# Mean squares and norm of a gate moved ahead of the first step of queries and keys, its norm weights into the second and third step

## The chip, the core and the metric

The kernel runs on one core of a Trainium2 chip. The metric is the device time of one execution in microseconds (us). The engines of a core work side by side, each through its own queue in order, and wait for one another by semaphores: PE (TensorE, matmuls), ACT (ScalarE), DVE (VectorE), POOL (GpSimd) and SP (which here only issues DMAs).

## What is computed

One decoder block on 1024 tokens of width 1024 in float32: eight heads of attention with a forget gate beside eight groups of a chunked spatial gate, then a gated MLP with a short convolution. The part that matters here, cut from the reference:

```
xn = rmsnorm(h, norm_mix_g)
proj = xn @ w_in                      # q, k, v (512 each), u, vg (512 each), 8 forget columns
log_f = log_sigmoid(proj[..., G_END:] + b_forget)
att = forgetting_attention(q, k, v, log_f)
uv = gelu(proj[..., V_END:G_END])     # u and vg
# chunked_spatial_gating, 8 groups of 64 columns:
vg = rmsnorm(vg, v_gain)              # mean square over the 64 columns of a group
mixed = einsum('gij,bnjgd->bnigd', tril(w_s), chunks_of_128(vg)) + b_s
sg = u * mixed
h = h + concat([att, sg]) @ w_out
```

The change touches the `rmsnorm` of `vg`: squares, their sums by group, the root, its reciprocal, the product with it (the norm) and the product with `v_gain` (the norm weights).

## The kernel before

The big products are done by Strassen-Winograd: matrices are cut into 2 x 2 blocks and seven block products take the place of eight (A11, A12, A22, S1 to S4 against B11, B21, T4, T1, T2, T3, B22). Each float32 operand is split into a high part and a low part (fp32r), and a product of two of them is three matmuls. A split is a cast on ACT and a subtraction on DVE (`split_w`, `tsplit`).

The order of the work around the change is this. First come the products for u, vg and the values (lines around 256), with a gelu on ACT at their end; `vgt[1]` and `vgt[0]` hold the two halves of vg (tokens 512 to 1023 and 0 to 511), each 128 partitions x 4 tiles x 512 columns, in G tiles. Then `forget` multiplies out the eight forget columns (L483), and `forget_sums` turns them into the running sums of log_f: L494 brings them into place, DVE and ACT alternate through the log-sigmoid (Exp, Ln), L507 and L508 multiply by a triangle and by ones, and a run of small adds on DVE follows.

Then come the four steps of queries and keys, `qk_step(i)` for i = 0 to 3, one for each 128 columns of weights. A step is seven products of 12 matmuls each (all on L400): qb (S2), qc (S3), qa (A12, for i > 0; its first product, A11, was made in the step before), qd (S1), qc again (A22, added onto the first), qa of the next step (A11), qd again (S4). Between them DVE combines the results out of PSUM. A product that adds onto qc or qd has to wait until DVE has read the bank. `emit` scales a result, splits it and stores it in `qd` or `kd` for the attention; its stores go out on SP. `nxt_of(i)` loads the next step's weights and makes their sums on POOL.

The gate's norm hangs in these steps. `gate_part(i)` of step i takes a quarter of vg: ACT squares 128 x 1024 elements into a pt tile, DVE sums them by groups of 64 into `gms`; in every second step ACT and DVE make root and reciprocal of 32 means, and one DVE instruction of 128 x 2048 elements norms the whole half. So half 1 is normed in step 1 and half 0 in step 3. `gate_gain(hf)` multiplies a half by the norm weights, 128 x 2048 in one instruction: half 1 in step 3, half 0 after the loop. The weights come by a DMA into a gg tile, issued at the first call.

After the loop, `vgs` splits the normed gate (eight casts into H tiles on ACT, eight subtractions on DVE), the second half of the values is multiplied out (`tmul` and `tprod`, L256, 96 matmuls), and `spatial` does the chunked gate (L661 to L663).

Who goes first is not simply the order of the code. A planner goes through the instructions in that order as their priority, simulates the engines with durations of its own, and on each engine takes the foremost instruction whose inputs and buffers are there; so an instruction can be put ahead of others that stand before it in the code if its engine would be idle. The result is a fixed queue for each engine. Tiles of one tag share a few buffers in turn: pt has three (used by `xu`, one for each step, by the squares and by a row of `scale_row`), gg two (`forget` uses both until `forget_sums` is done; one is used for the sums of each step's weights), H four, G four. All DVE and ACT instructions of this stretch are recorded under L43, a wrapper that also keeps them behind the end of the values' first part. So rows are told apart by their tiles: `gms<-pt` is the sum of squares, `gms<-gms` the root or reciprocal, `G<-G,gms` the norm, `G<-G,gg` the norm weights, `pt<-G` (ACT) the squares, `H<-G,H` the low part of the normed gate.

Of the kernel before, what the change touches and what calls it, by code (L numbers as in the profile page):

```python
# [11 lines left out]
AF = mybir.ActivationFunctionType  # L12
ALU = mybir.AluOpType
AX = mybir.AxisListType
P = 128
# [49 lines left out]
def block_kernel(ctx: ExitStack, tc: tile.TileContext, xT, xtok, wuv, wv, wqk, wf, cpk, bfv,  # L65
                 ggain, g2r, gfr, wsp, woa, wos, wup, wdn, out):
    nc = tc.nc
    act, dve, pool, pe, sp = Line(nc.scalar, tc), Line(nc.vector, tc), Line(nc.gpsimd, tc), nc.tensor, nc.sync
# [13 lines left out]
    def nm(s):  # L82
        uid[0] += 1
        return f"{s}_{uid[0]}"
# [6 lines left out]
    def sb(tag, shape, dt=F32):  # L91
        return (raws if tag == "raw" else late if tag in LATE else early).tile(shape, dt, tag=tag, bufs=BUFS[tag], name=nm(tag))
# [7 lines left out]
    def sbank():  # L100
        return psa.tile([P, 512], F32, tag="s", name=nm("ps"))

    def f32(ap):
        return ap.bitcast(F32)
# [6 lines left out]
    eps = cst.tile([P, 1], F32, name="eps")  # L111
# [85 lines left out]
    def ring(dt=F32R):  # L197
        rn[0] += 1
        return sb(RTAG[(rn[0] - 1) % 6], [P, 2, 512], dt)

    def psq(tag):
        return psa.tile([P, 512], F32, tag="b" if tag in "ab" else "s", bufs=4, name=nm("q" + tag))
# [29 lines left out]
    for p_ in range(2):  # L232
        t = sb("G", [P, 2, 2, 512])
# [3 lines left out]
    vgt = [sb("G", [P, 4, 512]) for _ in range(2)]  # L237
# [91 lines left out]
    for j in range(2):  # L329
        g = gb[2 * j:2 * j + 2]  # L330
# [64 lines left out]
    def product(ps, w, n, first):  # L395
        c = 0
        for k in range(4):
            ks = slice(k * P, (k + 1) * P)
            for wi, xi in ((0, 0), (0, 1), (1, 0)):
                pe.matmul(ps, w[:, wi, ks], xs(n, xi, k), start=(first and c == 0), stop=(c == 11),  # L400
                          skip_group_check=True)
                c += 1
# [85 lines left out]
    def forget_sums(c, r, zr):  # L488
        sel, bfb, z, e, rows = c[0:64, 128:136], c[:, 136:144], c[:, 144:208], c[:, 208:272], c[0:64, 272:400]
        tri, ones, lh, ll = r[:, 0:P], r[:, P:2 * P], r[:, 256:320], r[:, 320:384]  # L490
        v3 = lambda t: t.rearrange("p (h t) -> p h t", h=8)
        ps = sbank()
        for tt in range(8):
            pe.matmul(ps[:, tt * 8:(tt + 1) * 8], zr[:, tt * P:(tt + 1) * P], sel, start=True, stop=True)  # L494
        dve.tensor_tensor(out=v3(z), in0=ps[:, 0:64].rearrange("p (t h) -> p h t", h=8),
                          in1=rstd1.unsqueeze(1).to_broadcast((P, 8, 8)), op=ALU.mult)
        dve.tensor_tensor(out=v3(z), in0=v3(z), in1=bfb.unsqueeze(2).to_broadcast((P, 8, 8)), op=ALU.add)
        dve.scalar_tensor_tensor(out=e, in0=z, scalar=-1.0, in1=z, op0=ALU.mult, op1=ALU.max)
        act.activation(e, e, AF.Exp, scale=-1.0)
        act.activation(e, e, AF.Ln, bias=one[:, 0:1])  # L500
        dve.tensor_scalar(out=z, in0=z, scalar1=-1.0, scalar2=0.0, op0=ALU.mult, op1=ALU.max)
        dve.tensor_tensor(out=z, in0=z, in1=e, op=ALU.add)
        dve.tensor_copy(lh, z)
        dve.tensor_tensor(out=ll, in0=z, in1=f32(lh), op=ALU.subtract)

        for o, m in ((64, tri), (128, ones)):
            pe.matmul(ps[:, o:o + 64], m, lh, start=True, stop=False)  # L507
            pe.matmul(ps[:, o:o + 64], m, ll, start=False, stop=True)  # L508
        whole, run = v3(ps[:, 128:192]), v3(e)
        dve.memset(run[:, :, 0:1], 0.0)  # L510
        for tt in range(1, 8):
            dve.tensor_tensor(out=run[:, :, tt:tt + 1], in0=run[:, :, tt - 1:tt], in1=whole[:, :, tt - 1:tt], op=ALU.add)
        dve.tensor_tensor(out=v3(z), in0=v3(ps[:, 64:128]), in1=run, op=ALU.add)
        pe.transpose(ps[0:64, 192:320], z, ident)
        act.activation(rows, ps[0:64, 192:320], AF.Copy, scale=-1.0)
        sp.dma_start(out=ncd.rearrange("h (t p) -> (h t) p", p=P), in_=rows)
# [4 lines left out]
    def emit(t, dst, i, scale, parts):  # L521
        for o in parts:
            dve.scalar_tensor_tensor(out=t[:, 1, o], in0=t[:, 1, o], scalar=scale, in1=rb[:, o],
                                     op0=ALU.mult, op1=ALU.mult)
            act.copy(t[:, 0, o].bitcast(F32R), t[:, 1, o])
            dve.tensor_tensor(out=t[:, 1, o], in0=t[:, 1, o], in1=t[:, 0, o], op=ALU.subtract)
            for j in range(2):
                sp.dma_start(out=dst[2 * i + j].rearrange("s d t -> d s t")[:, :, o], in_=t[j * 64:(j + 1) * 64, :, o])

    gms = cst.tile([P, 64], F32, name="gms")  # L530

    def gate_part(i):

        hf, t = 1 - i // 2, 2 * (i % 2)
        sq = sb("pt", [P, 2, 512])
        act.activation(sq, vgt[hf][:, t:t + 2, :], AF.Square)
        r = gms[:, hf * 32 + t * 8:hf * 32 + t * 8 + 16]
        dve.tensor_reduce(out=r, in_=sq.rearrange("p t (g d) -> p (t g) d", d=64), axis=AX.X, op=ALU.add)
        if t:
            r = gms[:, hf * 32:hf * 32 + 32]  # L540
            act.activation(r, r, AF.Sqrt, bias=eps[:, 0:1], scale=1.0 / 64)
            dve.reciprocal(r, r)
            v3 = vgt[hf].rearrange("p t (g d) -> p (t g) d", d=64)
            dve.tensor_tensor(out=v3, in0=v3, in1=r.unsqueeze(2).to_broadcast((P, 32, 64)), op=ALU.mult)

    def nxt_of(i):
        if i == 3:
            while True:
                yield None
        w = Weights(i + 1)  # L550
        W.append(w)
        yield None
        w.split("A11")
        yield q1(i + 1, "a")
        w.sums()
        w.split("S2", "S3", "A12")
        w.last_sum()
        yield None
        yield None

    def qk_step(i, qa, nxt):
        w, t = W[i], xu[i]
        x1, u2 = t[:, 0, :], t[:, 1, :]
        qb = psq("b")
        product(qb, w.w["S2"], "T2", True)
        next(nxt)
        dve.tensor_tensor(out=u2, in0=qb, in1=x1, op=ALU.subtract)
        qc = psq("c")
        product(qc, w.w["S3"], "T3", True)
        dve.tensor_tensor(out=tk[:, 1, hi], in0=u2, in1=qc, op=ALU.subtract)  # L570
        w.split("S1")
        if i > 0:
            product(qa, w.w["A12"], "B21", False)
            act.copy(tq[:, 1, lo], qa)
        else:
            dve.tensor_tensor(out=tq[:, 1, lo], in0=q2, in1=x1, op=ALU.add)
        emit(tq, qd, i, -0.125, (lo,))
        w.split("A22")
        if i == 3:
            gate_gain(1)  # L580
        qd_ = psq("d")
        product(qd_, w.w["S1"], "T1", True)
        dve.tensor_tensor(out=tk[:, 1, hi], in0=tk[:, 1, hi], in1=qd_, op=ALU.subtract)
        gate_part(i)
        product(qc, w.w["A22"], "T4", False)
        dve.tensor_tensor(out=tk[:, 1, lo], in0=u2, in1=qc, op=ALU.subtract)
        emit(tk, kd, i, 1.0, (lo, hi))
        qa = next(nxt)
        w.split("S4")
        next(nxt)  # L590
        product(qd_, w.w["S4"], "B22", False)
        dve.tensor_tensor(out=tq[:, 1, hi], in0=qd_, in1=u2, op=ALU.subtract)
        emit(tq, qd, i, -0.125, (hi,))
        return qa

    gg = []

    def gate_gain(hf):
        if not gg:
            gg.append(sb("gg", [P, 512]))  # L600
            sp.dma_start(out=gg[0], in_=ggain.to_broadcast((P, 512)))
        dve.tensor_tensor(out=vgt[hf], in0=vgt[hf], in1=gg[0].unsqueeze(1).to_broadcast((P, 4, 512)), op=ALU.mult)

    W[0].split("S2", "S3")
    forget_sums(*fg)
    for i in range(4):
        qa = qk_step(i, qa, nxt_of(i))

# [2 lines left out]
    for k in range(4):  # L611
        t = sb("raw", [P, 2, 512])
# [4 lines left out]
    w0 = [tsplit(wvr[k][:, 0, :], True) for k in range(4)]  # L617


    gate_gain(0)  # L620
    vgs = [sb("H", [P, 2, 2, 8, 64], F32R) for _ in range(4)]
    for hf in (1, 0):
        for c in range(4):
# [18 lines left out]
    for p_ in range(2):  # L642
        t = ring(F32)
# [207 lines left out]
    def ut_(pool_, tag, shape, dt, bufs):  # L851
        return pool_.tile(shape, dt, tag=tag, bufs=bufs, name=nm(tag))
# [309 lines left out]
    for p_, n in ((upl, "B11"), (upl, "T2"), (upl, "B21"), (upl, "T3"), (upr, "T1"), (upr, "T4"), (upr, "B22")):  # L1162
        t = ut_(p_, "x" + n, [P, 2, 4, 512], F32, 1)
# [168 lines left out]
```

## Time and profile before

| | |
|---|---|
| median of 3 runs | 1097.8 us (1097.66 to 1100.26) |
| the profiled execution | 1102.1 us, span 1100.4 us |
| mean granted TensorE clock | 0.992 |
| busy | PE 97%, DVE 82%, ACT 52%, POOL 23% of the span |
| the four steps of queries and keys | about 118 to 198 us |

A row of a timeline gives start, duration, engine, line, operation, output <- inputs, shapes and count; a bracket at its end is the time that the engine sat idle before it, and who ended the wait. A row of a group has the count behind x, then busy time and mean ns of one, then idle time before. A row of a table of windows has start:end and length, then for PE, PEld, DVE, ACT and POOL the busy time (and instructions), then the granted TensorE clock (1.00 is full), the DMA engines' busy share and GB/s. In the page's line of shares of the chain, "issue" is time in which the engine waited for nothing that is recorded.

### The profile page before, as it was taken

Reading aid. Unit: us, or ns where it says so; the run is one execution under the profiler, and the core shown is the slowest. Engines: PE = TensorE matmul, PEld = TensorE weight load, DVE = VectorE, ACT = ScalarE, POOL = GpSimd, SP = SyncE. Lnnn points to the kernel's source line nnn. Section 1 sums busy time; section 2 is a strip of 40 time slices with the busy share of each in tenths; the row PEclk is TensorE's granted clock in tenths of the full one; section 3 lists DMA queues with packets and bytes.
Section 4 is the critical chain, followed back from the end, with each engine's and each line's share of the span. In section 5 each row is a group of like instructions: output and inputs, shape, how many; then the busy total and the mean of one; then the engine's idle time right before and its main releaser. Section 6 shows DMA issues by size and latency. Waiting matters only on the chain.

```text
span 1100.4 us, 14437 instructions
## 1 busy us (share of the span) xinstructions
PE 1070.2 (97%) x5013; PEld 880.7 (80%) x5013; DVE 897.8 (82%) x1355; ACT 572.2 (52%) x991; POOL 248.6 (23%) x205
## 2 busy tenths in 40 slices
PE   9999999999998999998999999999999999999997
PEld 6888787777877888776888888888888888888886
DVE  5985799775678859999898989999998875898774
ACT  5666544454467856653444444444444454454653
POOL 0002243133144341334232423333232000000000
PEclk9999999999998999999999999999999999999999
DMA  9242366836576345223133232313321898433342
GB/s 329 96 137 94 97 171 181 254 121 215 189 221 171 97 133 185 86 67 134 68 105 134 85 107 96 126 67 125 115 96 46 268 336 301 140 96 103 125 135 97
DMA packets 64713, 158.18 MB, mean 144 GB/s; under 512 B 7672, under 2 KB 7936, under 8 KB 64640
## 3 DMA queue, kind: packets, MB, share of 16 engines
q1 hardware_dynamic: 64352, 156.70, 43.7%
q8 instruction: 39, 0.64, 0.2%
q10 hardware_dynamic: 288, 0.56, 0.1%
q14 instruction: 34, 0.28, 0.1%
HBM read 114.95 MB, written 42.27 MB: 143 GB/s over the span
## 4 chain that ended last, share of the span: by engine, by line
PE 69%; DVE 7%; ACT 3%; issue 2%; DMA 2%; POOL 1%; SPq 0%; ACTq 0%; POOLq 0%; DVEq 0%
PE k L1189 18%; PE qa L999 10%; PE qd L999 10%; PE qc L999 10%; PE qb L999 5%; PE pb L759 3%; PE ps L256 2%; PE pb L749 2%; PE pf L803 1%; PE pf L804 1%; PE pf L802 1%; DMA x<-ncd 1%; PE ps L730 1%; PE ps L729 1%; DVE whb L159 1%
## 5 line engine op out<-in xcount | busy, mean ns | idle before, releaser
L1189 PE MATMUL k<-whb,wha 128*128 128x512 f32 x924 | 209.7, 389 | 0.0
L1189 PEld LDWEIGHTS k<-whb,wha 128*128 128x128 f32 x924 | 173.5, 188 | 36.1
L999 PE MATMUL qa<-xB,wha 128*128 128x512 f32 x528 | 128.9, 393 | 5.8 <-DVE wha L159 5.8
L999 PE MATMUL qc<-xT,whb 128*128 128x512 f32 x540 | 130.2, 390 | 1.4 <-DVE xT L930 1.4
L999 PEld LDWEIGHTS qa<-xB,wha 128*128 128x128 f32 x528 | 100.0, 190 | 27.4 <-DVE wha L159 6.6
L999 PEld LDWEIGHTS qc<-xT,whb 128*128 128x128 f32 x540 | 101.2, 188 | 23.2 <-DVE xT L930 1.8
L153 ACT CAST wha<-sg 128x512 fp32r<-128x512 f32 x77 | 47.9, 622 | 97.8 <-PE k L1189 87.0
L153 ACT CAST whb<-sg 128x512 fp32r<-128x512 f32 x85 | 51.9, 615 | 69.9 <-PE qc L999 67.7
L159 DVE TENSOR_TENSOR wha<-sg,wha 128x512 fp32r<-128x512 f32 x77 | 53.0, 690 | 40.8 <-ACT wha L153 40.6
L159 DVE TENSOR_TENSOR whb<-sg,whb 128x512 fp32r<-128x512 f32 x85 | 63.0, 743 | 9.1 <-ACT whb L153 8.9
L759 PE MATMUL pb<-pt,V 128*128 128x256 f32 (+1 forms) x320 | 59.4, 303 | 7.0 <-ACT pt L750 4.8
L999 PE MATMUL qd<-xB,whb 128*128 128x512 f32 x264 | 63.8, 389 | 0.1
L999 PE MATMUL qd<-xT,whb 128*128 128x512 f32 x264 | 63.4, 389 | 0.0
L759 PEld LDWEIGHTS pb<-pt,V 128*128 128x128 f32 x320 | 48.3, 194 | 18.6 <-ACT pt L750 11.5
L999 PE MATMUL qb<-xT,whb 128*128 128x512 f32 x252 | 61.0, 389 | 1.0 <-DVE whb L159 1.0
L750 ACT CAST pt<-pb 128x512 fp32r<-128x512 f32 (+1 forms) x80 | 40.8, 545 | 33.4 <-PE pb L749 32.7
L999 PEld LDWEIGHTS qd<-xB,whb 128*128 128x128 f32 x264 | 49.5, 188 | 10.7 <-issue 0.5
L999 PEld LDWEIGHTS qd<-xT,whb 128*128 128x128 f32 x264 | 49.6, 188 | 10.3
L751 DVE TENSOR_TENSOR pt<-pb,pt 128x512 fp32r<-128x512 f32 (+1 forms) x80 | 48.2, 632 | 10.9 <-ACT pt L750 10.2
L887 POOL TENSOR_TENSOR sg<-sg,raw 128x512 f32<-128x512 f32 x21 | 42.5, 2022 | 64.1 <-issue 61.6
L999 PEld LDWEIGHTS qb<-xT,whb 128*128 128x128 f32 x252 | 47.2, 188 | 11.1 <-DVE whb L159 1.4
L886 POOL TENSOR_TENSOR sg<-raw 128x512 f32<-128x512 f32 x21 | 30.6, 1458 | 110.0 <-DVE whb L159 85.6
(378 smaller groups left out, 2308.2 us busy)
## 6 DMA issues: line engine op xcount, KB each, us to landing
raw<-wup SPq DMA_DIRECT2D x44, 512.0 KB, 3.6
sg<-hx SPq DMA_DIRECT2D x77, 256.0 KB, 3.0
hx<-hs SPq DMA_DIRECT2D x44, 256.0 KB, 2.0
hx<-ca SPq DMA_DIRECT2D x33, 256.0 KB, 2.0
xT<-wdn SPq DMA_DIRECT2D x28, 256.0 KB, 4.8
raw<-wqk SPq DMA_DIRECT2D x8, 512.0 KB, 3.6
qd<-G SPq DMA_DIRECT2D x16, 256.0 KB, 4.7
kd<-G SPq DMA_DIRECT2D x16, 256.0 KB, 3.2
```

The source lines that it names most:

```text
L153: act.copy(h, src)
L159: return eng.tensor_tensor(out=l, in0=src, in1=f32(h), op=ALU.subtract)
L256: pe.matmul(banks[m], xs(n, xi, k)[:, ms], w[:, wi, :], start=(first and k == 0 and c == 0), stop=(k == 3 and c == 2), skip_group_check=True)
L729: pe.matmul(ps[:, 0:e - c], A[:, qs], B[:, c:e], start=True, stop=False)
L749: pe.transpose(ptr[:, c:c + P], tj[jj][:, k * P:(k + 1) * P], ident)
L750: act.copy(pt[:, 0, 0:w], ptr[:, 0:w])
L751: dve.tensor_tensor(out=pt[:, 1, 0:w], in0=ptr[:, 0:w], in1=f32(pt[:, 0, 0:w]), op=ALU.subtract)
L759: pe.matmul(po[:, oo:oo + n], lhs, pt[:, s, o:o + n], start=(k == 0 and s == 0), stop=(s == 1 and half))
L886: pool.tensor_tensor(out=s[0], in0=a21, in1=a22, op=ALU.add)
L887: pool.tensor_tensor(out=s[1], in0=s[0], in1=a11, op=ALU.add)
L999: pe.matmul(ps, w[:, wi, ks], xb[:, xi, k, :], start=(first and n == 0), stop=(n == 11), skip_group_check=True)
L1189: pe.matmul(banks[bk + m], xh[:, xi, ms], wh[:, wi, :], start=(first and p_ == 0 and n == 0), stop=(p_ == NP - 1 and n == 2), skip_group_c ...
```

## The change

`gate_part` becomes `gate_norm(hf)`, which does all of a half at once: two squares and two sums, root and reciprocal of the 32 means, and the norm as two instructions of 128 x 1024. It is called for half 1 ahead of `forget_sums` and for half 0 behind it, both ahead of the first step. `gate_gain` becomes two instructions of 128 x 1024 for each half; half 1 gets it in step 1 and half 0 in step 2, behind the subtraction of qd. The arithmetic is the same.

```diff
-    def gate_part(i):
-        hf, t = 1 - i // 2, 2 * (i % 2)
-        sq = sb("pt", [P, 2, 512])
-        act.activation(sq, vgt[hf][:, t:t + 2, :], AF.Square)
-        r = gms[:, hf * 32 + t * 8:hf * 32 + t * 8 + 16]
-        dve.tensor_reduce(out=r, in_=sq.rearrange("p t (g d) -> p (t g) d", d=64), axis=AX.X, op=ALU.add)
-        if t:
-            r = gms[:, hf * 32:hf * 32 + 32]
-            act.activation(r, r, AF.Sqrt, bias=eps[:, 0:1], scale=1.0 / 64)
-            dve.reciprocal(r, r)
-            v3 = vgt[hf].rearrange("p t (g d) -> p (t g) d", d=64)
-            dve.tensor_tensor(out=v3, in0=v3, in1=r.unsqueeze(2).to_broadcast((P, 32, 64)), op=ALU.mult)
+    def gate_norm(hf):
+        for t in (0, 2):
+            sq = sb("pt", [P, 2, 512])
+            act.activation(sq, vgt[hf][:, t:t + 2, :], AF.Square)
+            dve.tensor_reduce(out=gms[:, hf * 32 + t * 8:hf * 32 + t * 8 + 16],
+                              in_=sq.rearrange("p t (g d) -> p (t g) d", d=64), axis=AX.X, op=ALU.add)
+        r = gms[:, hf * 32:hf * 32 + 32]
+        act.activation(r, r, AF.Sqrt, bias=eps[:, 0:1], scale=1.0 / 64)
+        dve.reciprocal(r, r)
+        for t in (0, 2):
+            v3 = vgt[hf][:, t:t + 2, :].rearrange("p t (g d) -> p (t g) d", d=64)
+            dve.tensor_tensor(out=v3, in0=v3, in1=r[:, t * 8:t * 8 + 16].unsqueeze(2).to_broadcast((P, 16, 64)), op=ALU.mult)
...
     def qk_step(i, qa, nxt):
...
         w.split("A22")
-        if i == 3:
-            gate_gain(1)
         qd_ = psq("d")
         product(qd_, w.w["S1"], "T1", True)
         dve.tensor_tensor(out=tk[:, 1, hi], in0=tk[:, 1, hi], in1=qd_, op=ALU.subtract)
-        gate_part(i)
+        if i in (1, 2):
+            gate_gain(2 - i)
         product(qc, w.w["A22"], "T4", False)
...
     def gate_gain(hf):
...
-        dve.tensor_tensor(out=vgt[hf], in0=vgt[hf], in1=gg[0].unsqueeze(1).to_broadcast((P, 4, 512)), op=ALU.mult)
+        for t in (0, 2):
+            v = vgt[hf][:, t:t + 2, :]
+            dve.tensor_tensor(out=v, in0=v, in1=gg[0].unsqueeze(1).to_broadcast((P, 2, 512)), op=ALU.mult)
 
     W[0].split("S2", "S3")
+    gate_norm(1)
     forget_sums(*fg)
+    gate_norm(0)
     for i in range(4):
         qa = qk_step(i, qa, nxt_of(i))
...
-    gate_gain(0)
     vgs = [sb("H", [P, 2, 2, 8, 64], F32R) for _ in range(4)]
```

## The prediction

> **What bounds the kernel now.** I read the page first, then TensorE's own order of work around the change, then VectorE's for the same stretch.
>
> ```profile
> span 1100.4 us, 14437 instructions
> PE 1070.2 (97%) x5013; PEld 880.7 (80%) x5013; DVE 897.8 (82%) x1355; ACT 572.2 (52%) x991; POOL 248.6 (23%) x205
> PE 69%; DVE 7%; ACT 3%; issue 2%; DMA 2%; POOL 1%; SPq 0%; ACTq 0%; POOLq 0%; DVEq 0%
> ```
>
> TensorE is busy for 97% of the span and carries 69% of the chain that ended last. Work of other engines is worth only what it makes TensorE wait. So I looked for TensorE's waits in the four steps of queries and keys (118 to 198 us), and found them in the last of them, step 3:
>
> ```profile
> 181.39 2.88 PE L400 MATMUL qa<-x,whl 128*128 128x512 f32 x12
> 184.11 2.88 PE L400 MATMUL qd<-H,whl 128*128 128x512 f32 x12
> 187.69 3.01 PE L400 MATMUL qc<-V,whl 128*128 128x512 f32 x12 [0.70 <-DVE G L43]
> 193.67 4.23 PE L400 MATMUL qd<-t,whl 128*128 128x512 f32 x12 [2.98 <-DVE G L43]
> 219.89 0.39 PE L661 MATMUL pb<-H,wy 128*128 128x512 f32 x1
> ```
>
> One product of 12 matmuls takes 184.11 - 181.39 = 2.72 us start to start. From 184.11 to the first spatial matmul there are three products and the second values product of 96 matmuls, 11 times 12: 29.92 us at that rate. They took 35.78. The loss is 5.86 us, of which 0.70 + 2.98 = 3.68 are waits for VectorE. Most of the other 2.18 is clock:
>
> ```profile
> 190.00:193.60 3.60, 0.70 (x4) 0.23 (x2) 3.60 (x5) 1.24 (x3) 1.22 (x1) 1.00 0.98 349
> 193.60:196.00 2.40, 2.33 (x9) 1.90 (x10) 2.40 (x4) 2.12 (x5) 0.46 (x1) 0.81 0.15 61
> 196.00:198.00 2.00, 2.00 (x6) 1.61 (x5) 2.00 (x4) 0.99 (x2) 0.00 (x0) 0.50 0.73 147
> 198.00:200.00 2.00, 2.00 (x9) 1.56 (x9) 2.00 (x5) 0.62 (x1) 0.00 (x0) 0.88 0.88 230
> ```
>
> In these windows (start and end, length, busy time of PE, PEld, DVE, ACT and POOL, then the granted clock) the clock falls after the long wait: 0.19 of 2.40, half of 2.00 and 0.12 of 2.00 us make 1.70 us. VectorE is meanwhile busy without a gap. What it was doing:
>
> ```profile
> 142.26 3.38 DVE L43 TENSOR_TENSOR G<-G,gms 128x2048 f32<-128x2048 f32 x1
> 165.91 3.38 DVE L43 TENSOR_TENSOR G<-G,gg 128x2048 f32<-128x2048 f32 x1
> 180.33 1.22 DVE L43 TENSOR_REDUCE gms<-pt 128x16 f32<-128x1024 f32 x1 [0.27 <-ACT pt L43]
> 182.06 0.34 DVE L43 RECIPROCAL gms<-gms 128x32 f32<-128x32 f32 x1
> 182.86 2.28 DVE L43 TENSOR_TENSOR G<-G,gms 128x2048 f32<-128x2048 f32 x1
> 186.86 0.68 DVE L43 TENSOR_TENSOR G<-pt,qc 128x512 f32<-128x512 f32 x1
> 190.05 2.28 DVE L43 TENSOR_TENSOR G<-G,gg 128x2048 f32<-128x2048 f32 x1
> 192.85 0.68 DVE L43 TENSOR_TENSOR G<-G,qd 128x512 f32<-128x512 f32 x1
> ```
>
> The rows at 186.86 and 192.85 are the two subtractions for which TensorE waits (the read of qc ahead of the A22 product, the read of qd ahead of S4). The others are gate work: mean square, reciprocal, norm and norm weights. They sit on VectorE's queue in front of those subtractions, and nothing needs them before the spatial matmuls at 219.89.
>
> **The change, part by part.**
>
> *What leaves the last step.* Reduce 1.22, reciprocal 0.34 and norm 2.28, together 3.84 us, stood ahead of the first subtraction, and the weights of the other half, 2.28, between the two: 6.12 us ahead of the second. It ended at 193.53. The S4 product could start at 184.11 + 2 x 2.72 = 189.55. Without the 6.12 the subtraction would end at 187.41: 2.14 us of margin. Likewise the first, at 187.54, needs only 0.70 less and gets 3.84. What could eat the margin is work that the planner puts into the freed time: the splits of the normed gate are ready sooner, and two of the four H tiles come free early in the last step, so four splits of this row's 0.68 us could move ahead:
>
> ```profile
> L43 DVE TENSOR_TENSOR H<-G,H 128x512 fp32r<-128x512 f32 x8 | 5.1, 683 | 0.0
> ```
>
> They are 2.73 us against 2.14, a rest of 0.6 us at worst. I take 0.5 of the 5.86 as not recovered: 5.4 us gained, with ends at 2.2 (second rival) and 5.86.
>
> *What steps 1 and 2 get.* The weights now come as two halves per step. From the rows above, 2048 elements take 2.28 and 512 take 0.68 us, so 1024 take some 1.21. With contention the row at 165.91 sets the other end, 3.38 / 2 = 1.69. Four halves: 4.8 to 6.8 us. What goes from 138 to 186 us is a norm 3.38, weights 3.38, two reduces and two reciprocals (3.12) and a norm of 2.28: 12.2 us. So VectorE, with 43.83 of 48 us busy there (row below), gets lighter in each case. I count nothing for it on TensorE, which has no wait there.
>
> ```profile
> 143.45 3.34 POOL L424 TENSOR_TENSOR raw<-raw 128x512 f32<-128x512 f32 x1
> 121.18 1.81 POOL L422 TENSOR_TENSOR raw<-raw,raw 128x512 f32<-128x512 f32 x1 [18.82 <-DVE whl L43]
> ```
>
> The first row says why the norm at 142.26 took 3.38 and the one at 182.86 2.28: GpSimd was adding at the same time and was slowed too. The second says that GpSimd is idle for 18.8 us before 121.18, where the norms now go, so there they should cost the shorter time. The Trainium skill ("SBUF — State Buffer", section "SBUF: two separate sides") has it that an add with two SBUF inputs and a GpSimd operation take turns for one pair of ports, each for a whole instruction; the trace agrees (1.10 us more at 142.26), and by it each moved norm is worth up to that much more than its count.
>
> *What the front gets.* Part 0's reduce is done at 112 already (rows below). Added are three reduces (3.66), two reciprocals (0.68) and four half norms (4 x 1.21 = 4.84): 9.2 us on VectorE. Their cover is its idle time, 16.00 - 9.04 = 6.96 us:
>
> ```profile
> 110.00:126.00 16.00, 15.21 (x73) 10.37 (x71) 9.04 (x17) 8.47 (x13) 3.09 (x2) 1.00 0.30 99
> 126.00:138.00 12.00, 12.00 (x56) 9.87 (x56) 11.39 (x24) 6.55 (x12) 2.88 (x2) 1.00 0.37 92
> 138.00:186.00 48.00, 48.00 (x213) 39.49 (x212) 43.83 (x52) 22.08 (x38) 18.07 (x10) 1.00 0.61 168
> 112.04 1.22 DVE L43 TENSOR_REDUCE gms<-pt 128x16 f32<-128x1024 f32 x1 [0.71 <-ACT pt L43]
> 120.28 0.23 DVE L43 TENSOR_TENSOR gg<-ps,rstd 128x64 f32<-128x64 f32 x1 [3.91 <-PE ps L494]
> 126.78 0.69 DVE L43 TENSOR_TENSOR G<-pt,qc 128x512 f32<-128x512 f32 x1
> 125.56 0.30 PE L507 MATMUL ps<-gg 128*128 128x64 f32 x1 [0.79 <-DVE gg L43]
> 129.35 2.88 PE L400 MATMUL qc<-V,wy 128*128 128x512 f32 x12
> ```
>
> The excess is 2.3 us, and VectorE is full from 126 on. The subtraction at 126.78, which ends at 127.47, may slip 1.88 us before the A22 product at 129.35 is late. So 0.4 us reach TensorE. Ahead of that stands the chain of the forget gate: from 120.28 on VectorE and ScalarE hand four small results to and fro until L507, which holds up everything behind it on TensorE. Each hand-over can meet a gate instruction already running, at worst a reduce of 1.22. The bounds run from -0.8 (the present 0.79 us wait goes) to the first rival's 9.0; I take 0.6, half a reduce, since the forget gate stands ahead of the second half's norm in the code. Together the front costs 1.0 us. Waits that short leave the clock at 1.00, as in the first two windows.
>
> ```profile
> L43 ACT ACTIVATE pt<-G 128x1024 f32<-128x1024 f32 x4 | 4.2, 1062 | 0.3 <-issue 0.3
> L43 ACT ACT_TABLE_LOAD x3 | 3.8, 1283 | 0.1
> L43 ACT ACTIVATE gms<-gms,eps 128x32 f32<-128x32 f32 x2 | 0.6, 322 | 0.8 <-DVE gms L43 0.8
> ```
>
> ScalarE gets three squares (3.2), two roots (0.6) and one or two table loads (1.3 to 2.6) in the first window, where it is idle for 7.5 us. They fit. A second load comes if the second root falls behind the forget gate's Exp and Ln.
>
> *Queues.* The change issues no new DMA. The load of the norm weights moves from the end of step 1 to its middle or before, behind step 0's stores on SP, and takes a gg slot that the forget gate frees; the stores behind it feed only the attention, which comes after the spatial stage. GpSimd's sums share the two gg slots, one of which is now held longer; the sums of one step (from 121.18) and of the next (its third at 143.45) lie some 20 us apart, so I count nothing.
>
> *Sum.* -5.4 + 1.0 = -4.4 us. Nothing after 198 us hangs on a fixed time: the values product, the spatial stage and the attention follow TensorE. The profiled execution took 1102.1 us (span 1100.4), the median of the runs 1097.8; I take the 4.4 from both: 1097.7 for the profiled one, 1093.4 us for the median.
>
> **The rivals.**
>
> *The forget gate waits (slower).* If the whole second half lands inside the forget gate's chain, L507 waits for two reduces 2.44, a table load 1.28, a root 0.32, a reciprocal 0.34 and two half norms 2.42: 6.8 us, and 2.18 for the clock as at 196 us, 9.0. Net +3.6: 1101.4 us. It turns slower once that wait grows by more than 3.2 us. For it: the chain is the only thing for which TensorE waits there now. Against: its small operations come first in the code, and VectorE's 3.91 us of idle time stand just ahead of it. 0.11.
>
> *The freed time fills up again.* If other early splits or contention keep a wait of 2 us ahead of S4, the clock goes too:
>
> ```profile
> 354.09 0.39 PE L759 MATMUL pb<-pt,V 128*128 128x256 f32 x1 [2.25 <-ACT pt L750]
> 355.00:360.00 5.00, 5.00 (x30) 4.71 (x28) 4.20 (x13) 2.31 (x7) 3.10 (x3) 0.66 0.00 0
> ```
>
> A wait of 2.25 us cost 0.34 of 5 us, 1.7. Then 5.86 - 2.0 - 1.7 - 1.0 = 1.2 us are gained: 1096.6. Against: only two H tiles are free then. 0.14.
>
> *No clock to win.* If the unprofiled runs lose only the waits, 3.68 - 1.0 = 2.7 us are gained: 1095.1. The Trainium skill ("TensorE: Matmul & The Clock Gate", section "What's actually happening") lets the clock drop only after an idle window of about 3.4 us, counted freely, so a 2.98 us gap would not do it; the two drops shown here came after 2.98 and 2.25 us and speak against that. 0.08.
>
> *Nothing moves.* The planner, which already ran part 0 at 112, leaves the rest where VectorE's order had it: 1097.8. 0.05.
>
> **How the numbers follow.** My forecast has 0.62; its own range is 1091.9 to 1094.4, from the gain of 5.86 with no cost to one of 3.4. A measurement of this kernel can tell about 0.3%, 3.3 us, from no change. Faster by more is my forecast alone, 0.62. Within 0.3% are the second to fourth rivals, 0.27, slower the first, 0.11. The range goes from 1091.2 (5.86 and the 0.79 wait at L507 too) to 1098.6, which takes in all but the first rival and a little scatter.
>
> **What would show it.** Right: gms rows all before some 130 us; no bracket of over 0.7 us at the last A22 and S4 products; clock 1.00 around 190 to 200; first L661 some 4 us earlier, near 215.5. The front's cost stands in the bracket at L507 and at the first A22 product. It is wrong if L507 waits over 3 us, if gate or H rows still lie between the last two subtractions with TensorE waiting, or if the 4 us are there at 220 and gone at the end.

## The result, and the profile after

The change makes the kernel slower. The comparison of the two gives a ratio of 1.0052 with a 95% interval of 1.0035 to 1.0069, some 5.7 us more where 4.4 less were forecast. The medians of six runs each, 1105.6 us against 1098.5 us, lie 7.1 us apart. The profiled execution after took 1105.2 us, span 1103.5 (1100.4 before). Its busy times:

```profile
PE 1070.5 (97%) x5013; PEld 878.9 (80%) x5013; DVE 896.1 (81%) x1359; ACT 573.3 (52%) x992; POOL 247.6 (22%) x205
```

TensorE does the same work (1070.5 us busy, 1070.2 before) in a longer span. To find where, I cut the stretch of the change at four starts on TensorE: the A11 product of step 0 (104.29 in before, 104.75 after), the S1 products of steps 1 and 3, and the first spatial matmul. They are called front, middle and tail here:

| us | front | middle | tail | whole stage |
|---|---|---|---|---|
| before | 41.53 | 38.29 | 35.78 | 115.60 |
| after | 46.31 | 39.73 | 34.17 | 120.21 |
| difference | +4.78 | +1.44 | -1.61 | +4.61 |

So 4.61 us are lost in the stage, most of them in the front. The rest of the difference is not to be read from one execution: from the spatial stage to the first up product the profiled runs of all kernels here lie between 227.4 and 234.1 us (before at 232.6, after at 230.7), and only 2.7 us of that has a cause in a kernel's own changes (the last run below).

TensorE's timeline after shows the places (the bracket is the wait ahead of a row; PEld is the load of a product's weights):

```profile
127.61 0.19 PE L507 MATMUL ps<-gg 128*128 128x64 f32 x1
133.93 0.70 PE L400 MATMUL qd<-t,whl 128*128 128x512 f32 x2 [1.81 <-DVE gg L43]
136.45 4.06 PE L400 MATMUL qa<-V,whl 128*128 128x512 f32 x10 [1.50 <-DVE whl L43]
140.43 2.19 PEld L400 LDWEIGHTS qd<-t,whl 128*128 128x128 f32 x10 [0.64 <-DVE whl L43]
179.82 2.97 PE L400 MATMUL qd<-t,whl 128*128 128x512 f32 x12 [1.40 <-DVE G L43]
190.79 2.88 PE L400 MATMUL qd<-H,whl 128*128 128x512 f32 x12
193.81 3.00 PE L400 MATMUL qc<-V,whl 128*128 128x512 f32 x12
198.70 2.99 PE L400 MATMUL qd<-t,whl 128*128 128x512 f32 x12 [1.88 <-DVE G L43]
205.10 3.69 PE L256 MATMUL ps<-wy,x 128*128 128x512 f32 x15 [1.38 <-DVE G L43]
224.96 0.39 PE L663 MATMUL pb<-H,wy 128*128 128x512 f32 x1
```

The wait at the last A22 is nearly gone (193.81 is 0.30 more than 2.72 after 190.79), and the one at the last S4 fell from 2.98 to 1.88. But a wait of 1.38 has come at the first bank of the values product, one of 1.40 at S4 of step 2, and two of 1.81 and 1.50 in step 0, where before had none. L507, where I had looked for the price, waits for nothing now. The windows (columns as before) show the clock:

```profile
110.46:126.46 16.00, 16.00 (x77) 11.24 (x75) 10.61 (x18) 13.00 (x19) 0.00 (x0) 1.00 0.20 66
136.50:139.00 2.50, 2.50 (x7) 1.96 (x8) 2.50 (x3) 0.00 (x0) 2.40 (x2) 0.63 0.41 96
199.00:205.00 6.00, 4.72 (x21) 3.57 (x19) 6.00 (x10) 2.27 (x5) 0.09 (x1) 1.00 0.84 221
```

After the two waits of step 0 the clock is 0.63; in the last step it is now 1.00. The first row shows where the front's loss begins: ScalarE is busy for 13.00 of these 16 us (8.47 in the same stretch before) and VectorE for 10.61 (9.04). What fell behind is a pair of weight splits: one for the A11 product that step 0 makes for step 1, one for S4 of step 0. ScalarE's casts in before, and then after:

```profile
117.90 0.62 ACT L43 CAST whl<-raw 128x512 fp32r<-128x512 f32 x1
120.33 0.62 ACT L43 CAST whl<-raw 128x512 fp32r<-128x512 f32 x1 [1.82 <-PE ps L494]
```

```profile
118.47 1.28 ACT L43 ACT_TABLE_LOAD   x1
119.77 0.32 ACT L43 ACTIVATE gms<-gms,eps 128x32 f32<-128x32 f32 x1
122.38 1.04 ACT L43 ACTIVATE pt<-G 128x1024 f32<-128x1024 f32 x1
123.44 1.28 ACT L43 ACT_TABLE_LOAD   x1
124.99 1.13 ACT L43 CAST whl<-raw 128x512 fp32r<-128x512 f32 x2
```

Squares (from 115.73 on), loads and a root fill the gaps in which the casts stood; both come together at 124.99. Their subtractions on VectorE in before, and then VectorE's rows of step 0 and of the last step after:

```profile
120.42 0.68 DVE L43 TENSOR_TENSOR whl<-raw,whl 128x512 fp32r<-128x512 f32 x1
121.15 0.69 DVE L43 TENSOR_TENSOR whl<-raw,whl 128x512 fp32r<-128x512 f32 x1
```

```profile
130.00 1.23 DVE L43 TENSOR_TENSOR G<-G,gms 128x1024 f32<-128x1024 f32 x1
131.22 1.22 DVE L43 TENSOR_TENSOR G<-G,gms 128x1024 f32<-128x1024 f32 x1
133.11 0.68 DVE L43 TENSOR_TENSOR G<-G,qd 128x512 f32<-128x512 f32 x1
135.71 0.69 DVE L43 TENSOR_TENSOR whl<-raw,whl 128x512 fp32r<-128x512 f32 x1
138.61 1.76 DVE L43 TENSOR_TENSOR whl<-raw,whl 128x512 fp32r<-128x512 f32 x1
188.48 2.18 DVE L43 TENSOR_TENSOR H<-G,H 128x512 fp32r<-128x512 f32 x2
192.39 0.68 DVE L43 TENSOR_TENSOR H<-G,H 128x512 fp32r<-128x512 f32 x1
194.69 0.68 DVE L43 TENSOR_TENSOR H<-G,H 128x512 fp32r<-128x512 f32 x1
197.27 0.68 DVE L43 TENSOR_TENSOR H<-G,H 128x512 fp32r<-128x512 f32 x1
197.87 0.68 DVE L43 TENSOR_TENSOR G<-G,qd 128x512 f32<-128x512 f32 x1
204.37 0.68 DVE L43 TENSOR_TENSOR G<-qd,pt 128x512 f32<-128x512 f32 x1
```

Four things can be read here. The two splits are some 15 and 17 us later than before (135.71 and 138.61), and the first ends just when TensorE goes on with A11 at 136.45. The second ends at 140.37, and S4's weights are loaded 0.06 us later, at 140.43; A11's ten matmuls, slow by the clock, last until then, so the slow clock hides a wait for this split. The read of qd at 133.11 stands behind the half norms of half 0 at 130.00 and 131.22; S4 starts 0.14 us after its end. The profile names gg as the releaser, a small row of the forget gate on the same queue that ends 0.07 us before S4 starts. In the last step four rows of H splits, 188.48 to 197.27, stand ahead of the read of qd at 197.87: five splits of the gate that nobody needs before 224.96. And the read of the last product at 204.37 is what the values product waits for at 205.10.

### The profile page after: what moved, and what is told of

It is laid out like the page before. It is cut to its first block, busy times and chain, and to the rows that moved or that the text cites. A ratio compares the mean times of both kernels' runs of the same rounds, so it can differ in the third digit from the quotient of the medians.

```text
span 1103.5 us, 14439 instructions
## 1 busy us (share of the span) xinstructions
PE 1070.5 (97%) x5013; PEld 878.9 (80%) x5013; DVE 896.1 (81%) x1359; ACT 573.3 (52%) x992; POOL 247.6 (22%) x205
## 4 chain that ended last, share of the span: by engine, by line
PE 80%; DVE 9%; ACT 4%; DMA 3%; issue 3%; POOL 1%; SPq 0%; ACTq 0%; POOLq 0%; DVEq 0%
PE k L1191 18%; PE qd L1001 10%; PE qa L1001 9%; PE qc L1001 9%; PE ps L256 6%; PE pb L256 5%; PE qb L1001 5%; PE pb L761 2%; DVE G L43 2%; PE qa L400 2%; PE qd L400 1%; PE pb L751 1%; PE pf L805 1%; PE pf L804 1%; PE pf L806 1%
```

## The experiments

Four questions: is it ScalarE's queue or VectorE's load that makes the front late; do the H splits take the freed time in the tail; is gate work the cause of the old tail at all; and where can half 0 go. `after(tc, a, b)`, the kernel's own helper, keeps instruction a behind b. All runs in one table; ratio to the kernel before with its interval (a run without one was profiled only):

| run | front | middle | tail | stage | ratio |
|---|---|---|---|---|---|
| half 0 normed in step 1 | 42.33 | 40.33 | 35.59 | 118.25 | 1.0022 (1.0009 to 1.0036) |
| roots behind Ln | 41.95 | 39.59 | 35.74 | 117.28 | 1.0009 (0.9993 to 1.0026) |
| no half norms | 42.53 | 38.08 | 35.01 | 115.62 | |
| H splits held | 46.22 | 39.62 | 31.70 | 117.54 | 1.0035 (1.0012 to 1.0058) |
| roots behind Ln, splits held | 41.93 | 39.59 | 33.54 | 115.06 | 1.0023 (1.0006 to 1.0039) |
| before, weights of half 0 held | 41.52 | 38.30 | 35.78 | 115.60 | 1.0000 (0.9986 to 1.0015) |
| before, these and splits held | 41.51 | 38.28 | 35.62 | 115.41 | 1.0013 (1.0002 to 1.0025) |
| before, no gate work of half 0 | 41.51 | 38.09 | 30.72 | 110.32 | |
| before, half 0 behind values | 41.51 | 38.18 | 33.69 | 113.38 | 0.9989 (0.9975 to 1.0003) |
| that, with part 3's sum | 41.48 | 38.34 | 33.13 | 112.95 | 0.9979 (0.9963 to 0.9994) |
| that, with parts 2 and 3 | 42.08 | 38.08 | 31.04 | 111.20 | 0.9984 (0.9969 to 0.9999) |

### The front: one half less

```diff
...
+        if i == 1:
+            gate_norm(0)
         if i in (1, 2):
             gate_gain(2 - i)
...
     forget_sums(*fg)
-    gate_norm(0)
```

> The changed kernel with the whole norm of half 0 (two squares, two sums, root, reciprocal, two half norms) called in step 1, just ahead of the weights of half 1, instead of ahead of step 0. Half 1 and all weights stay as changed. Measured as the stretch from the first A22 product to the second step's S2 product (8.31 us before, 14.24 changed, 8.16 with TensorE never waiting) and from the first A11 product of step 0 to the first spatial matmul (115.60 before, 120.21 changed). Theory 'half 0 in front is too much' (its squares, second root and norms push the splits of the next A11 and S4 weights back): the first stretch falls to 8.2 to 9.5, the time falls by 4 to 5 us against the changed kernel, to within 1 us of before. Rival 'half 1 alone does it' (its root between the forget gate's functions): the first stretch stays above 11.

The front falls from 46.31 to 42.33, the ratio from 1.0052 to 1.0022. That is some 3.3 us where 4 to 5 were expected, for middle and tail are worse (40.33 and 35.59): the norm of half 0 now stands in step 1, among the steps again. One half ahead of the steps is nearly free, two are not; whether by ScalarE or VectorE this run alone doesn't say.

### The front: the roots behind the forget gate's Ln

All four squares and sums stay in front; both roots go together behind Ln, and the half norms with them.

```diff
-    gate_norm(1)
-    forget_sums(*fg)
-    gate_norm(0)
+    gate_sums(1)
+    exp_ln = forget_sums(*fg)
+    gate_sums(0)
+    gate_norm(1)
+    gate_norm(0)
...
-        act.activation(r, r, AF.Sqrt, bias=eps[:, 0:1], scale=1.0 / 64)
+        after(tc, act.activation(r, r, AF.Sqrt, bias=eps[:, 0:1], scale=1.0 / 64), exp_ln)
```

> The changed kernel with both halves' squares and sums still in front, but both roots, reciprocals and norms behind the forget gate's logarithm on ScalarE, the two roots together. VectorE's gate work in front is the same; ScalarE loads three function tables instead of four and has its casts free before Exp. Theory 'ScalarE's queue' (the roots' table loads hold up the casts of the next A11 and S4 weights, so VectorE's halves of these splits fall behind the gate work): the first stretch (14.24 changed) falls below 10.5. Rival 'VectorE's load' (some 6.7 us of gate work after 122 us wherever it stands): it stays above 12.

VectorE has the same work ahead of step 1 as after, yet the front is 41.95. ScalarE's timeline, then VectorE's:

```profile
119.40 0.60 ACT L43 CAST whl<-raw 128x512 fp32r<-128x512 f32 x1
121.57 0.62 ACT L43 CAST whl<-raw 128x512 fp32r<-128x512 f32 x1 [1.57 <-PE ps L494]
126.73 0.53 ACT L43 ACTIVATE gms<-gms,eps 128x32 f32<-128x32 f32 x2
```

```profile
123.88 1.29 DVE L43 TENSOR_TENSOR whl<-raw,whl 128x512 fp32r<-128x512 f32 x2
135.34 0.68 DVE L43 TENSOR_TENSOR G<-G,qd 128x512 f32<-128x512 f32 x1
```

The casts are back at 119.40 and 121.57, the splits at 123.88, ahead of the norms. The read of qd is even later than after's (135.34 against 133.11), and TensorE has other products to run meanwhile, since the A11 weights are there and the planner puts the next step's S2 first. So the load of VectorE alone does not make the loss; the order in which ScalarE releases the splits does, together with what then stands on VectorE's queue (the next run). The planner's new order of products is a part of this that I did not separate.

### The front: without the half norms

This kernel leaves out the four half norms of after, so the gate goes on unnormed.

```diff
-        for t in (0, 2):
-            v3 = vgt[hf][:, t:t + 2, :].rearrange("p t (g d) -> p (t g) d", d=64)
-            dve.tensor_tensor(out=v3, in0=v3, in1=..., op=ALU.mult)
```

> The changed kernel without the four half norms on VectorE (4.9 us in front; the gate is left unnormed); squares, sums, roots and reciprocals stay, and with them ScalarE's queue and the place of the next A11 and S4 weight splits behind the forget gate's logarithm. If the place alone made the wait, the stretch from the first A22 product to the second step's S2 product stays above 12 us (14.24 changed). If it takes the place and VectorE's load in front of it together, it falls by about the 4.9 us, to 9 to 10.

```profile
135.42 0.30 PE L514 MATMUL ps<-ident,gg 128*64 128x128 f32 x1 [0.85 <-DVE gg L43]
136.43 0.74 PE L400 MATMUL qc<-x,whl 128*128 128x512 f32 x2 [0.24 <-ACT whl L43]
137.58 2.57 PE L400 MATMUL qd<-t,whl 128*128 128x512 f32 x10 [0.17 <-DVE whl L43]
194.03 2.97 PE L400 MATMUL qd<-t,whl 128*128 128x512 f32 x12 [3.29 <-DVE G L43]
```

In TensorE's front the two waits of 3.31 us together have become three short ones of 1.26 us (0.85 of them at L514, a row of the forget gate), front 42.53, although the two casts on ScalarE still start only at 124.72. Here too the planner puts parts of the next step's products first, so the stretch that the expectation names can't be compared as it stands. So it is enough to take the norms away, or to have the casts in their old place: by these two runs the loss takes both, late casts and a full queue on VectorE behind them.

The last row bears on the tail: though no norm is left anywhere in the steps, S4 of step 3 waits 3.29 us, and the tail is 35.01. Five H splits (from 183.22 to 191.54) stand ahead of its read of qd.

### The tail: the H splits held

```diff
-        dve.tensor_tensor(out=tq[:, 1, hi], in0=qd_, in1=u2, op=ALU.subtract)
+        ends.append(dve.tensor_tensor(out=tq[:, 1, hi], in0=qd_, in1=u2, op=ALU.subtract))
...
-            dve.tensor_tensor(out=l, in0=src, in1=f32(h), op=ALU.subtract)
+            after(tc, dve.tensor_tensor(out=l, in0=src, in1=f32(h), op=ALU.subtract), ends[3])
```

> The changed kernel with VectorE's eight splits of the normed gate (H tiles) ordered behind the last subtraction of step 3; nothing else changed. Measured from the last S1 product's start to the first spatial matmul (35.78 us before, 34.17 changed, 29.92 with no loss). Theory 'the freed time is filled again' (six H splits, 4.6 us, stand ahead of the last subtraction of qd): this stretch falls to 30 to 31.5, and the time by about 3 us against the changed kernel, still slower than before by 1.5 to 3. Rival 'VectorE is behind anyway' (late from the front and from contention with GpSimd): it stays above 33.

```profile
195.50 2.88 PE L400 MATMUL qd<-t,whl 128*128 128x512 f32 x12
201.89 3.72 PE L256 MATMUL ps<-wy,x 128*128 128x512 f32 x15 [1.47 <-DVE G L43]
```

S4 of step 3 has no bracket any more and the tail is 31.70, 2.5 us less than after: the splits did take the freed time. The whole time is not shown to have fallen with it: 1.0035 has an interval that overlaps that of 1.0052. What is left is the wait for the bank that the last subtraction reads.

The same with the roots behind Ln was to bring both gains together:

> The two repairs together: the changed kernel with both roots and norms behind the logarithm, and the eight H splits on VectorE behind the last subtraction of step 3. If the front's loss comes from the late weight splits and the last step's from the H splits put into the freed time, the stretch from the first A11 product of step 0 to the first spatial matmul falls from 120.21 us (changed) and 115.60 (before) to 112.5 to 114, and the time to 2 to 3 us below before (ratio 0.997 to 0.9985). If VectorE's lateness from contention with GpSimd is what counts, that stretch stays above 115.

It did not. The stage is 115.06, not under 114, with waits of 1.17 and 1.78 at the values product, and the ratio of 1.0023 is some 3 us worse than this stage explains. That remains open. The profiled execution took 1098.7 us, 4.0 less than this kernel's median, so its trace need not show what the others lost; in the two other kernels that hold all eight splits the time also lies 1.6 to 1.9 us above what the stage gives, and no wait in the hundred us behind the stage shows it.

### Before, with the same holds

Gate weights of half 0 behind the last subtraction, nothing else moved:

```diff
...
-    gate_gain(0)
+    after(tc, gate_gain(0), ends[3])
...
```

> The kernel before with one edit: the norm weights of half 0 ordered behind the last subtraction of step 3 instead of between the two subtractions for which TensorE waits. Theory 'gate work in front of the subtractions makes the last step's waits': the wait of 2.98 us ahead of the last S4 product falls below 1, the clock stays at full speed, the stretch from the last S1 product to the first spatial matmul falls from 35.78 to about 32, the time by 3 to 4 us (ratio 0.9965 to 0.9975). Rival 'the wait moves on' (the values product then waits for its banks or for its weights): under 1 us gained.

The time is the same to the measurement, and so is the tail, 35.78. VectorE's timeline says why:

```profile
190.17 0.68 DVE L43 TENSOR_TENSOR H<-G,H 128x512 fp32r<-128x512 f32 x1
191.98 0.68 DVE L43 TENSOR_TENSOR H<-G,H 128x512 fp32r<-128x512 f32 x1
193.18 0.68 DVE L43 TENSOR_TENSOR G<-G,qd 128x512 f32<-128x512 f32 x1
```

Where 2.28 us of weights stood, two splits stand now, and the read of qd ends at 193.86, 9.45 us after the S1 product's start at 184.41; in before it was 9.42. The two splits, 1.36 us, are not all of it: a weight split at 186.58, beside a GpSimd sum, takes 1.57 instead of 0.68, so that A22's wait grows from 0.70 to 1.60 us, and two more rows of the step's own work (191.38 and 192.58) come ahead of the read. With all eight splits held as well:

> The kernel before with the norm weights of half 0 and all eight H splits on VectorE ordered behind the last subtraction of step 3. In the run with the weights alone held, two H splits took their place and the stretch stayed at 115.60. Theory 'whatever is ready fills the time': with nothing left to fill it, the stretch from the last S1 product to the first spatial matmul falls from 35.78 to 31.5 to 33 us (the norm of half 0 still stands there), the time by 3 to 4 us (ratio 0.9965 to 0.9975). Rival 'the wait moves on' to the weights of the values product or its banks: above 34.5 us and no gain.

```profile
188.76 3.01 PE L400 MATMUL qc<-V,whl 128*128 128x512 f32 x12 [1.42 <-DVE G L43]
192.83 3.00 PE L400 MATMUL qd<-t,whl 128*128 128x512 f32 x12 [1.07 <-DVE G L43]
199.12 3.70 PE L256 MATMUL ps<-wy,x 128*128 128x512 f32 x15 [1.25 <-DVE G L43]
209.27 5.53 PE L256 MATMUL ps<-wy,t 128*128 128x512 f32 x23 [0.78 <-DVE wy L43]
```

TensorE's timeline has four waits instead of two, and the tail is 35.62: with norm and sum of half 0 still ahead of the last subtractions, the wait moves from one to the next, as the rival had it.

### Before, without half 0's gate work

Squares, sums, root, norm and weights of half 0 are left out, the splits held.

> The kernel before without the gate work of half 0 (squares, sums, root, norm and weights left out), its eight H subtractions held behind the last subtraction of step 3. Theory (gate work makes the last step late): the tail from S1(3) to the spatial stage takes 31 to 32 us, both waits under 0.7 us. Rival (VectorE is behind in that step by its own combining work and weight splits): over 34 us, with a wait of over 1 us for a subtraction or a split.

```profile
189.31 2.88 PE L400 MATMUL qd<-t,whl 128*128 128x512 f32 x12
194.75 3.69 PE L256 MATMUL ps<-wy,x 128*128 128x512 f32 x15 [0.51 <-DVE G L43]
```

Tail 30.72, 0.8 us over the 29.92 of TensorE alone. Holding weights and splits, with the work still done, left 35.62 (the run before), so the gate work of half 0 is what the last step loses by once nothing fills its place: 5.06 us less than before in the tail, of the 5.86 that I had counted. Both are needed, less work and nothing in its place: in the changed kernel without the half norms, its splits free to move up, the tail was 35.01.

### Half 0 behind the values product

In the run just shown VectorE idles for 2.35 and 2.50 us ahead of its rows at 204.97 and 213.49, behind the values product's splits. Root, norm, weights and splits of half 0 go there; the four splits of half 1 are held behind the last subtraction.

```diff
-        if t:
+        if t and hf:
+            gate_root(hf)
+    def gate_root(hf):
...
+        if not hf:
+            after(tc, rc, ends[3])
...
     tprod(S, lambda k: wvr[k][:, 1, :], "B22", False)
+    gate_root(0)
+    gate_gain(0)
+    gate_split(0)
     spatial()
```

> The kernel before, with half 0's root, reciprocal, norm and weights emitted behind the splits of the values product (reciprocal held behind the last subtraction of step 3) and all eight H subtractions held behind that subtraction as well. Theory (the last step is late because gate work stands ahead of its two subtractions, and filling work takes the place of whatever leaves): with both kept out, S1(3) to the first spatial matmul takes 31.5 to 33 us, as with the held splits (31.7), and the stage (first A11 to spatial) 111.5 to 113 us; ratio 0.9965 to 0.998. Rival (the wait moves on to what VectorE then owes: the bank of the values product, the normed half 0, the H splits): a wait of over 1 us at the values product or the first spatial matmuls, that tail over 34.5, ratio 0.999 to 1.001.

Tail 33.69, between the two expectations; stage 113.38; the ratio, 0.9989, is not told from no change. A wait of 1.49 stays at S4 and one of 1.69 at the values product. VectorE's timeline has the sum of part 3 still there (181.02), and two instructions of 0.68 us elsewhere that take 1.50 and 1.77 beside GpSimd's sums at 186.18 and 187.82:

```profile
181.02 1.22 DVE L43 TENSOR_REDUCE gms<-pt 128x16 f32<-128x1024 f32 x1 [0.27 <-ACT pt L43]
186.53 1.50 DVE L43 SCALAR_TENSOR_TENSOR wy<-raw,wy 128x512 fp32r<-128x512 f32 x1
187.96 1.77 DVE L43 SCALAR_TENSOR_TENSOR G<-G,t 128x512 f32<-128x512 f32 x1
```

So part 3's square and sum were moved as well (`if i < 3: gate_part(i)` in the step, part 3 ahead of `gate_root(0)`):

> The run with half 0 behind the values product, and the last quarter's square and sum (part 3) moved there too. Theory (gate work on VectorE ahead of the last subtractions is what makes the last step late): the sum of 1.22 us at 181.02 goes from ahead of them, the wait of 1.49 at S4 falls under 0.7 and the tail to 31 to 32.5 us, the stage to 110.7 to 112.2; ratio 0.995 to 0.998. Rival (the two GpSimd sums beside VectorE's subtractions at 186 to 189 make it late whatever stands ahead): the S4 wait stays over 1 us, tail over 33, ratio 0.998 to 1.0.

This is narrowly faster than before, 0.9979 (0.9963 to 0.9994), about 2.3 us, as the stage's -2.65 has it. The wait at S4 is 0.94, so the sum's 1.22 us are only partly won; the values product still waits 1.70, and the tail of 33.13 is the rival's, not the theory's. Two of VectorE's rows beside GpSimd's sums still take 1.64 and 1.77. With part 2 moved too (the last run):

> As the run before, with part 2's square and sum behind the values product as well. Theory: nothing more is gained in the four steps (no wait in step 2 to take away), stage within 0.5 us of the run with part 3 alone, ratio 0.995 to 0.998, unless the spatial stage waits: half 0 is then 7.3 us of VectorE work behind some 198 us and its splits come at about 215 us, when the first spatial matmuls start. Rival (VectorE's work in step 2 still pushes step 3): tail 0.5 us or more shorter than with part 3 alone.

```profile
221.95 0.47 PE L676 MATMUL pb<-H,wy 128*128 128x512 f32 x1 [2.71 <-DVE A L43]
```

The tail shrinks by a further 2.1 us, against my expectation that step 2 does not matter: VectorE reaches the subtraction of qb 3.9 us before S1 instead of 0.7. S4 of step 3 has no wait, though two rows beside GpSimd's sums still take 1.48 and 1.78; so by these two runs that contention makes the step late only where VectorE has no lead to lose. But on TensorE's timeline the spatial matmuls wait 2.71 us, as the expectation had it for its exception: VectorE's last four H splits run from 215.04 to 219.04, and its first row that empties a spatial bank starts behind them, at 220.94. The gain is given back; the ratio, 0.9984 (0.9969 to 0.9999), cannot be told from the run before it.

## Why the prediction was wrong, step by step

**The front, put at 1.0 us, cost 4.78.** This step failed. Both prices lay at the wrong place: L507 waits for nothing after, and the first A22 was not late either. The cost is the two waits, 1.81 and 1.50, and some 1.7 by which A11's ten matmuls took longer than at 2.72 us for twelve (S4's split would have held TensorE that long in any case), less the 0.79 that L507 no longer waits; half a microsecond I did not trace. I had compared sums, 9.2 us of new work with 6.96 of idle time on VectorE (2.2 too much, not 2.3), and 7.5 us on ScalarE ("They fit"). They did fit by their sums: ScalarE was busy 13.00 of 16. But the idle time was no single piece. It lay between the casts and subtractions for A11 and S4, and a product waits for each of these. Squares, loads and roots ahead of the casts, and half norms ahead of the subtractions, moved the subtractions by 15 and 17 us. I had looked for who waits for the forget gate and not listed what else those queues carried for step 0. The durations were right: half norms 1.22 and 1.23 against 1.21.

**Steps 1 and 2, put at nothing, cost 1.44.** The count of nothing for the queues failed with it. GpSimd's sums of the next weights come behind the A11 split: the first starts at 136.53, 0.13 us after that split's end (the profile names a cast on ScalarE that ends 0.04 us later), and stood at 121.18 before. By the trace this delay is handed on: in step 2 VectorE waits for the cast of a GpSimd sum until 173.95, and two GpSimd adds then run beside its rows ahead of S4's read of qd; S4 waits 1.40. That S4's wait stays with the H splits held (1.24) and is absent without the half norms, and with the roots behind Ln, fits this reading; it was not isolated, and with the roots behind Ln the middle is hardly shorter, 39.59, for a wait of 1.25 comes in step 1.

**The last step, put at 5.4 us of gain, gave 1.61.** The size of the loss was right: without half 0's gate work 5.06 of the tail come back. The clock's part came back: it is 1.00 there now. The step that failed is the price of the splits that move up, four of them with 0.5 us not recovered: five came ahead of the read of qd, 2.18 + 3 x 0.68 = 4.22 us against a margin of 2.14, and the wait behind it, at the values product's bank, was not on my list. One of the prediction's own signs of being wrong came with it, H rows between the last two subtractions with TensorE waiting. The second rival had this mechanism, but priced the clock with it, which did not fall; its 1.2 us of total gain still rested on the cheap front. Holding the splits brought 2.5 of the missing 3.8.

**The rivals.** The first rival had the sign, by a wait at L507 that did not come. No rival held what came: late weight splits for the A11 and S4 products at the end of step 0.

**The sum.** +4.78 + 1.44 - 1.61 = +4.61 us in the profiled pair; the comparison of all runs gives 5.7, with an interval of 3.8 to 7.6.

## What to carry to other kernels

Idle time on an engine is no cover until it is known which small instructions already live between its gaps: list each queue's rows in the window, with the next one who waits for each, before comparing sums. Where a planner fills queues by priority, work taken out of the way is replaced by whatever is ready; the freed time has to be held for the instruction it was meant for, and the next wait on the same chain priced as well. Here the two versions that came out faster, by about 2 us, took half 0's norm out of the four steps to the other side, behind the values product, where VectorE was idle and nobody waits for it until the spatial stage.

## What the runs showed of the hardware

The length of a wait does not by itself tell whether the granted clock falls. After, two waits of 1.81 and 1.50 us, with 1.0 us of matmuls between, brought it to 0.63, while a lone 1.88 us (at 198.70) left it at 1.00. In before a wait of 2.98 us brought it to 0.50, as did one of 2.48 with the roots behind Ln (ahead of 200.65). But the 3.29 us ahead of S4 in the kernel without the half norms left it at 1.00 (first row), and in the last run it was 0.50 while TensorE was busy throughout, with no wait ahead of it (second row):

```profile
192.00:197.00 5.00, 2.97 (x13) 2.52 (x14) 5.00 (x7) 1.20 (x3) 2.24 (x2) 1.00 0.78 213
122.00:124.00 2.00, 2.00 (x6) 1.56 (x5) 1.97 (x4) 1.16 (x2) 1.88 (x2) 0.50 0.06 18
```

The Trainium skill ("TensorE: Matmul & The Clock Gate", section "What's actually happening") has the clock drop after an idle window of about 3.4 us. Here waits of 2.98 and 2.48 were enough, so less than a whole window did it, and for the drop without a wait these traces show no cause; the last run's front, in which it falls, is 0.6 us longer than that of the run before it.

A table load took 1.28 us, the root behind it started 0.02 us after its end (118.47, 119.77) and ended at 120.09, and the next load followed at 120.11. The Trainium skill ("ScalarE: Activation LUTs", section "What ACT_TABLE_LOAD costs") adds some 1.38 us of drain to each switch; no such gap stands at the loads shown here.
